# Expert stage of a two-block transformer kernel: instructions held in program order, one-hot tiles built in pairs two groups ahead

## The chip, the cores and the metric

The kernel runs on one core of one Trainium2 chip. The metric is device time in microseconds (us) of one execution. The engines are PE (TensorE, matrix products; PEld is its loading of weights), DVE (VectorE), ACT (ScalarE), POOL (GpSimd) and SP (SyncE, which here only issues DMAs). DMAs issued by SP go through queue q1, those issued by POOL through queue q0.

## The reference, cut to what matters

The program computes a first block (convolution and windowed attention, then a PEER expert layer) and a second block of two layers. Only the expert layer of the first block is touched:

```python
def peer(h, w_pq, sub_keys, u_emb, v_emb):
    ...
    s_top, i_top = lax.top_k(sc, PEER_TOPK)
    cand = s_top[..., 0, :, None] + s_top[..., 1, None, :]
    ...
    best, pos = lax.top_k(cand, PEER_TOPK)
    expert_idx = jnp.take_along_axis(cand_idx, pos, axis=-1)
    gate = jax.nn.softmax(best, axis=-1).astype(h.dtype)
    ...
    def chunk(args):
        hx, idx, g = args
        a = jax.nn.gelu(jnp.einsum("ced,cd->ce", u_emb[idx], hx), approximate=False)
        return jnp.einsum("ce,ced->cd", g * a, v_emb[idx])
```

There are 256 tokens, 8 heads with 16 chosen experts each (128 experts for a token), 16384 experts, and a width of 1024 in float32.

## The kernel before, in words

**Two ways for two sets of tokens.** 160 of the 256 tokens (N = 160) go the dense way: every expert is computed, and a mostly empty gate matrix picks the chosen ones. 128 blocks of 128 experts pass through `ublock`, which loads one tile of 512 KB of the first table (`ut`), multiplies it in 8 matmuls with the activations `hn`, and leaves gelu of the product in the tile `G`. In the same way 128 blocks of the second table (`vv`) are multiplied with G in `vmm`. The other 96 tokens go by rows: `RowGroup` fetches for each of 64 and then 32 steps a tile of 128 rows (512 KB) by an indirect DMA from POOL, `dot` multiplies it with the activations on DVE (first table), `axpy` adds it to a sum on DVE (second table). That is 192 row tiles: 96 of `un`, 96 of `vv`. `some_rows(RU)` after a U block and `some_rows(RV)` after a V block say how many steps of this come into the program per block; a row is used RB - 1 steps after its fetch.

**Three stretches.** First `ublock`s that alternate with what is left of the top-16 selection (`unit`, `select`, `gates`), which `pump` doles out to DVE by estimated costs; tokens 128 to 255 (tt = 1) come first, then tokens 0 to 127 (tt = 0). `gates` computes the softmax and, in `turn`, transposes indices and gates with PE; for tt = 1 `turn` also fills the row indices and sets `asked`, from which on rows are fetched. Second, the placing: for 40 groups of 4 tokens `onehots` builds one-hot tiles (QO on DVE, P and R from it on ACT), `place` multiplies them on PE (8 matmuls of 128 columns) into a gate tile in PSUM, and multiplies that gate into G (on DVE for the blocks already done, a copy on ACT for those to come). From then on a `ublock` multiplies its gelu with the gates already placed (`ac`, on DVE). Some two U blocks stand between groups. Third, the 128 V blocks, the last 5 of them interleaved with the adding of the row groups' sums.

**Order and buffers.** `whole` loads all blocks from SP into a ring of 10 tiles named raw, whi and wlo; a tile is free once PE has used its block. U products use 4 PSUM tiles ("mm"). A scheduler of the framework takes the program and decides the order on each engine; each engine then works strictly in that order.

Of the kernel before, what the change touches and what calls it, by code (L numbers as in the profile page):

```python
# [17 lines left out]
PSUM = bass.MemoryType.PSUM  # L18
DRAM = bass.MemoryType.DRAM
# [55 lines left out]
RU = 0.68  # L75
RV = 0.8

# [7 lines left out]
RB = 6  # L85


class Kernel:
    def __init__(self, tc, a, dump=None):
        self.tc, self.nc, self.a = tc, tc.nc, a  # L90
        self.dump = dump or (lambda *k: None)
        self.es = ExitStack()
        self.pools = {}
        self.wt = 0
        self.bg = []
        self.credit = 0.0
        self.lag = []

# [700 lines left out]
    def peer(self):  # L799
# [11 lines left out]
        gTl = p2h.tile([128, T], F32, name="gTl")  # L811
# [118 lines left out]
        def gates(tt):  # L930
            at = lambda t: t[:, tt]
            nc.vector.scalar_tensor_tensor(at(ei), at(isel), float(N_KEYS), at(jsel), op0=ALU.mult, op1=ALU.add)
            nc.vector.tensor_tensor(at(ex), at(best), best[:, tt, :, 0:1].to_broadcast([128, 8, 16]), op=ALU.subtract)
            nc.scalar.activation(at(ex), at(ex), AF.Exp)
            sm = p2t.tile([128, 8], F32, name="sm", bufs=1)
            nc.vector.reduce_sum(sm, at(ex), axis=AX.X)
            nc.vector.reciprocal(sm, sm)
            nc.vector.tensor_mul(at(ex), at(ex), sm[:, :, None].to_broadcast([128, 8, 16]))
            ts = slice(tt * 128, (tt + 1) * 128)
# [12 lines left out]
            self.later(1, turn)  # L952
            yield 1.5
# [19 lines left out]
        def whole(src, n):  # L973
# [3 lines left out]
            nc.sync.dma_start(raw, src)  # L977
            return raw

        def G(i, t=slice(None)):  # L980
            return Gs[i // 64][:, i % 64, t]

        def ublock(i, n_t):
            raw = whole(a["ut"][i], i)
            pt = self.pp.tile([128, N], F32, name="mm", bufs=4)
            for k in range(C):
                nc.tensor.matmul(pt, raw[:, k * 128:(k + 1) * 128], hn[:, k, :N], start=(k == 0), stop=(k == C - 1))  # L987
            self.tick()
# [44 lines left out]
        done, i = 0, 0  # L1033
        while self.bg:
# [5 lines left out]
        for _ in range(2):  # L1040
            ublock(i, 0)
            some_rows(RU)
            i += 1
# [53 lines left out]
        for i in range(64 - LAST):  # L1097
            blk = (i, whole(a["vv"][i], nv))
# [422 lines left out]
class RowGroup:  # L1521
# [3 lines left out]
    def __init__(self, k, pool, hn, ei, ex, t0, n):  # L1525
# [5 lines left out]
        self.idx = pool.tile([128, n], I32, name=f"idx{t0}")  # L1531
        self.gate = pool.tile([128, n], F32, name=f"gate{t0}")
# [3 lines left out]
        nc.vector.reduce_sum(self.fold, k.ident.rearrange("p (c t) -> p t c", t=n), axis=AX.X)  # L1536

# [16 lines left out]
    def indices(self):  # L1554

        nc, k = self.k.nc, self.k
        tt = self.t0 // 128
        pt = k.pp.tile([128, 2, 128], F32, name="ax", bufs=4)
        for j, src in enumerate(self.src):
            nc.tensor.matmul(pt[:, j], self.spread, src[:, tt].rearrange("p a b -> p (a b)"), start=True, stop=True)  # L1560
        for c in range(self.copies):
            ps = slice(c * self.n, (c + 1) * self.n)
            nc.vector.tensor_copy(self.idx[ps], pt[ps, 0, ps])
            nc.vector.tensor_copy(self.gate[ps], pt[ps, 1, ps])
# [222 lines left out]
```

## Time and profile before

| what | value |
|---|---|
| three runs | 1698.18, 1698.95 (median), 1701.84 us |
| the profiled execution | 1699.78 us, its span 1698.0 us |
| PE, DVE, ACT, POOL busy | 93%, 68%, 40%, 25% of the span |
| mean granted TensorE clock | 0.968 |
| moved by DMA | 398.98 MB, 235 GB/s over the span |

The span is the time from the first to the last instruction of the profiled execution; 1.8 us lie around it. "Busy" for PE does not mean working at its peak. All times below that name a moment are microseconds from the span's start. The expert stage's U blocks begin at 344.3, its gate placing at 480.7, its V blocks at 754.3, and its last adding ends at about 1043.

### The profile page before, as it was taken

Reading aid. Unit: us, or ns where it says so; the run is one execution under the profiler, and the core shown is the slowest. Engines: PE = TensorE matmul, PEld = TensorE weight load, DVE = VectorE, ACT = ScalarE, POOL = GpSimd, SP = SyncE. Lnnn points to the kernel's source line nnn. Section 1 sums busy time; section 2 is a strip of 40 time slices with the busy share of each in tenths; the row PEclk is TensorE's granted clock in tenths of the full one; section 3 lists DMA queues with packets and bytes.
Section 4 is the critical chain, followed back from the end, with each engine's and each line's share of the span. In section 5 each row is a group of like instructions: output and inputs, shape, how many; then the busy total and the mean of one; then the engine's idle time right before and its main releaser. Section 6 shows DMA issues by size and latency. Waiting matters only on the chain.

```text
span 1698.0 us, 29932 instructions
## 1 busy us (share of the span) xinstructions
PE 1577.1 (93%) x11502; PEld 1488.8 (88%) x11502; DVE 1155.1 (68%) x2510; ACT 678.3 (40%) x1549; POOL 430.4 (25%) x308
## 2 busy tenths in 40 slices
PE   8989989979667898979999999999999999999998
PEld 7878879979667788879999999887999998799986
DVE  6989988999777888884500005965777666676754
ACT  4557545531144454420000004455555444554543
POOL 3734622604554556663300000100000011000000
PEclk9989989989879999999999999999999999999999
DMA  5523436548999999999997774642655567265553
GB/s 182 171 75 101 137 124 216 158 174 334 357 356 408 408 409 400 409 392 410 409 338 241 246 227 155 224 137 75 210 194 186 183 191 221 90 191 180 182 190 113
DMA packets 109390, 398.98 MB, mean 235 GB/s; under 512 B 12484, under 2 KB 12643, under 8 KB 108736
## 3 DMA queue, kind: packets, MB, share of 16 engines
q1 hardware_dynamic: 78336, 282.63, 48.7%
q0 software_dynamic: 30768, 114.39, 17.9%
q8 instruction: 90, 1.47, 0.4%
q14 instruction: 52, 0.43, 0.1%
q10 hardware_dynamic: 144, 0.07, 0.0%
HBM read 394.86 MB, written 6.11 MB: 236 GB/s over the span
## 4 chain that ended last, share of the span: by engine, by line
PE 60%; DVE 18%; DMA 14%; issue 4%; POOL 2%; ACT 1%; SPq 0%; DVEq 0%; POOLq 0%; ACTq 0%
PE ax L1077 14%; PE mm L147 11%; PE mm L148 11%; PE mm L149 11%; DMA row<-un,idx 6%; DMA row<-vv,idx 4%; PE mm L987 2%; DVE ax L591 2%; PE mm L215 1%; PE mm L213 1%; PE ax L444 1%; PE mm L214 1%; DVE junk L1573 1%; DVE acc L1583 1%; DMA wlo<-vv 1%
## 5 line engine op out<-in xcount | busy, mean ns | idle before, releaser
L124 ACT ACTIVATE whi<-raw 128x1024 fp32r<-128x1024 f32 x275 | 290.2, 1058 | 602.3 <-DMA raw<-wst 287.6
L128 DVE TENSOR_TENSOR wlo<-raw,whi 128x1024 fp32r<-128x1024 f32 x211 | 257.9, 1224 | 277.9 <-ACT whi L124 271.6
L147 PE MATMUL mm<-xgh,whi 128*128 128x256 f32 x1064 | 304.4, 286 | 0.0
L148 PE MATMUL mm<-xgl,whi 128*128 128x256 f32 x1064 | 301.5, 283 | 2.6 <-DVE xgl L387 2.6
L149 PE MATMUL mm<-xgh,wlo 128*128 128x256 f32 x1064 | 301.2, 283 | 0.4 <-DVE wlo L128 0.4
L148 PEld LDWEIGHTS mm<-xgl,whi 128*128 128x128 f32 x1064 | 202.2, 190 | 2.9 <-DVE xgl L387 2.8
L147 PEld LDWEIGHTS mm<-xgh,whi 128*128 128x128 f32 x1064 | 202.0, 190 | 1.1 <-issue 0.8
L149 PEld LDWEIGHTS mm<-xgh,wlo 128*128 128x128 f32 x1064 | 202.1, 190 | 0.7 <-DVE wlo L128 0.6
L126 POOL TENSOR_TENSOR wlo<-raw,whi 128x1024 fp32r<-128x1024 f32 x64 | 153.5, 2403 | 138.1 <-ACT whi L124 135.3
L1583 DVE SCALAR_TENSOR_TENSOR acc<-row,w,acc 128x1024 f32<-128x1024 f32 x94 | 120.8, 1285 | 62.5 <-DMA row<-vv,idx 62.1
L1568 POOL DMA_INDIRECT row<-un,idx x96 | 113.7, 1185 | 148.7 <-PE mm L987 57.0
L1568 POOL DMA_INDIRECT row<-vv,idx x96 | 121.6, 1266 | 107.1 <-DVE acc L1583 61.2
L1573 DVE CUSTOM_DVE_ANT_0 junk<-row,h 128x1024 f32<-128x1024 f32 x96 | 117.5, 1224 | 43.6 <-DMA row<-un,idx 39.0
L987 PE MATMUL mm<-hn,raw 128*128 128x160 f32 x816 | 125.5, 311 | 3.4 <-ACT G L995 3.1
L987 PEld LDWEIGHTS mm<-hn,raw 128*128 128x128 f32 x816 | 117.9, 198 | 8.9 <-ACT G L995 7.2
L1077 PE MATMUL ax<-G,raw 128*128 128x160 f32 x832 | 122.6, 300 | 0.2
L1077 PEld LDWEIGHTS ax<-G,raw 128*128 128x128 f32 x832 | 115.7, 190 | 0.8 <-DMA raw<-vv 0.7
L987 PE MATMUL mm<-hn,whi 128*128 128x160 f32 x624 | 96.4, 310 | 16.0 <-ACT G L990 11.0
L987 PEld LDWEIGHTS mm<-hn,whi 128*128 128x128 f32 x624 | 90.2, 197 | 22.9 <-ACT G L990 11.3
L148 PE MATMUL mm<-hl,whi 128*128 128x256 f32 x368 | 107.2, 291 | 2.2 <-DVE hl L358 2.1
L987 PE MATMUL mm<-hn,wlo 128*128 128x160 f32 x608 | 93.7, 309 | 15.8 <-ACT G L990 12.7
L987 PEld LDWEIGHTS mm<-hn,wlo 128*128 128x128 f32 x608 | 87.8, 197 | 20.0 <-ACT G L990 12.9
(433 smaller groups left out, 3430.7 us busy)
## 6 DMA issues: line engine op xcount, KB each, us to landing
raw<-wst SPq DMA_DIRECT2D x278, 512.0 KB
raw<-vv SPq DMA_DIRECT2D x52, 512.0 KB
raw<-ut SPq DMA_DIRECT2D x51, 512.0 KB
whi<-ut SPq DMA_DIRECT2D x39, 512.0 KB
wlo<-ut SPq DMA_DIRECT2D x38, 512.0 KB
wlo<-vv SPq DMA_DIRECT2D x38, 512.0 KB
whi<-vv SPq DMA_DIRECT2D x38, 512.0 KB
tabr<-tabd POOLq DMA_DIRECT2D x1, 2048.0 KB
```

The costliest lines, as they stand in the source:

```text
L124: nc.scalar.activation(hi, raw, AF.Copy)
L126: nc.gpsimd.tensor_sub(lo, raw, hi)
L128: self.pin = nc.vector.tensor_sub(lo, raw, hi)
L147: nc.tensor.matmul(pt, w[:, s], xs[0][:, k], start=first, stop=False)
L148: nc.tensor.matmul(pt, w[:, s], xs[1][:, k], start=False, stop=False)
L149: nc.tensor.matmul(pt, lo[:, s], xs[0][:, k], start=False, stop=last)
L591: nc.vector.scalar_tensor_tensor(y[:, c] if k == 30 else ps, u[:, c, k:k + T], cw[:, c, k:k + 1], ps, op0=ALU.mult, op1=ALU.add)
L987: nc.tensor.matmul(pt, raw[:, k * 128:(k + 1) * 128], hn[:, k, :N], start=(k == 0), stop=(k == C - 1))
L1077: nc.tensor.matmul(acc[d // 2][:, d % 2, :N], raw[:, d * 128:(d + 1) * 128], G(i), start=False, stop=False, skip_group_check=True)
L1568: self.k.nc.gpsimd.indirect_dma_start(t, None, table, bass.IndirectOffsetOnAxis(ap=self.idx[:, s:s + 1], axis=0))
L1573: self.k.nc.vector.tensor_tensor_reduce(junk, row, self.h, 1.0, 0.0, ALU.mult, ALU.add, self.a[:, s:s + 1])
L1583: self.k.nc.vector.scalar_tensor_tensor(self.acc, row, w, self.acc, op0=ALU.mult, op1=ALU.add)
```

## The change

Everything lies in the expert stage. A context `in_order` ties each instruction of an engine to the one before it in the program (an order without a semaphore), from the first `ublock` to the end of the V loop. RU goes from 0.68 to 0.8, the row buffers RB from 6 to 8. The steps of `gates` come 2, 3 and 4 blocks after its first two DVE operations (GL), the row indices (`pick(0)`) apart from the row gates (`pick(1)`). One-hots are built with two tokens next to each other in the innermost dimension; R is made by POOL in one operation for a group, no longer by 4 operations on ACT; they are built two groups ahead of their use. `put`, the second half of the old `place`, runs one block later, and the product with `ac` one block later too (3 `ac` buffers). Of the V blocks each one whose number is divisible by 4 is loaded from POOL, not SP.

```diff
-RU = 0.68
+RU = 0.8
...
+GL = (2, 3, 4)
...
-RB = 6
+RB = 8
...
+    @contextmanager
+    def in_order(self):
+        traced = self.nc.cur_bb.bb.instructions
+        start = traced[-1]
+        yield
+        traced = list(self.nc.cur_bb.bb.instructions)
+        n = next(k for k in reversed(range(len(traced))) if traced[k] is start)
+        last = {}
+        for ins in traced[n:]:
+            if ins.engine in last and ins.engine in PINNED:
+                self.tc.add_manual_dep(ins, last[ins.engine].name, mybir.DependencyInfo(
+                    mybir.DependencyClass.NoSync, mybir.DependencyReason.DATA), reason="in_order")
+            last[ins.engine] = ins
...
+            if tt == 1:
+                self.later(GL[0], ask)
+            for n, fn in zip(GL, (exp, softmax, turn)):
+                self.later(n, fn)
...
-                nc.vector.tensor_mul(G(i, slice(0, n_t)), G(i, slice(0, n_t)), ac[:, :n_t])
+                muls.append((G(i, slice(0, n_t)), ac[:, :n_t]))
...
-            QO = oh.tile([128, 2, NT, 128], F16, name="QO", bufs=3)
-            P, R = (oh.tile([128, NT, 128], F16, name=n, bufs=2) for n in ("P", "R"))
-            nc.vector.tensor_tensor(QO, io[:, None, None, :].to_broadcast([128, 2, NT, 128]),
-                                    jiT[:, :, ts, None].to_broadcast([128, 2, NT, 128]), op=ALU.is_equal)
+            QO = oh.tile([128, 2, NT // 2, 128, 2], F16, name="QO", bufs=3)
+            P, R = (oh.tile([128, NT // 2, 128, 2], F16, name=n, bufs=3) for n in ("P", "R"))
+            for p in range(NT // 2):
+                ps = slice(t0 + 2 * p, t0 + 2 * p + 2)
+                nc.vector.tensor_tensor(QO[:, :, p], io[:, None].to_broadcast([128, 2, 128, 2]),
+                                        jiT[:, :, None, ps].to_broadcast([128, 2, 128, 2]), op=ALU.is_equal)
             for k in range(NT):
-                for dst, g in ((P, gT), (R, gTl)):
-                    nc.scalar.activation(dst[:, k], QO[:, 1, k], AF.Copy, scale=g[:, t0 + k:t0 + k + 1])
...
+            nc.gpsimd.tensor_tensor(R, QO[:, 1], gTl[:, t0:t0 + NT].rearrange("p (a b) -> p a b", b=2)[:, :, None].to_broadcast([128, NT // 2, 128, 2]), op=ALU.mult)
...
+        ohs = [onehots(4 * g, poh, io) for g in range(2)]
+        done, pts = 0, []
         for g in range(n_g):
...
+            if g + 2 < n_g:
+                ohs.append(onehots(4 * (g + 2), poh, io))
+            while i < i0 + 1 + (g + 1) * (126 - i0) // n_g:
                 ublock(i, 4 * done)
                 some_rows(RU)
+                products(1)
                 i += 1
...
+            pts.append(place(4 * g, ohs.pop(0)))
...
-            blk = (i, whole(a["vv"][i], nv))
+            blk = (i, whole(a["vv"][i], nv, nc.gpsimd if nv % 4 == 0 else nc.sync))
```

**ACT at the start.** Rows of ACT around the two exponentials of `gates` (`ex`), between the gelu operations (`G<-mm`, one per U block), before:

```order
L934 ACTIVATE ex<-ex 128x128
L990 ACT_TABLE_LOAD
L990 ACTIVATE G_4197<-mm 128x160 x8
L949 ACTIVATE jiT<-ax 128x2x128
L950 ACTIVATE gT<-ax 128x128
L357 ACTIVATE gTh<-gT 128x128
L990 ACTIVATE G_4197<-mm 128x160 x13
L934 ACT_TABLE_LOAD
L934 ACTIVATE ex<-ex 128x128
```

The same place of the change:

```order
L1023 ACTIVATE G_4197<-mm 128x160 x11
L962 ACT_TABLE_LOAD
L962 ACTIVATE ex<-ex 128x128
L1023 ACT_TABLE_LOAD
L1023 ACTIVATE G_4197<-mm 128x160 x2
L976 ACTIVATE jiT<-ax 128x2x128
L977 ACTIVATE gT<-ax 128x128
L376 ACTIVATE gTh<-gT 128x128
L1023 ACTIVATE G_4197<-mm 128x160 x22
L962 ACT_TABLE_LOAD
L962 ACTIVATE ex<-ex 128x128
```

The first exponential stood behind 3 gelus and stands behind 11 now; the second stood 21 gelus later and stands 24 later now. On PE the products that need the row indices stand behind 11 U blocks before and 12 now, the second transposes behind 36 and 38, and the first placing behind 40 and 41.

**DVE in the placing.** Rows of DVE about two groups long (`junk` is a row's dot product, QO the one-hots, `G<-ax` the placed gates, `G<-G,ac` the product of a U block), before:

```order
L1573 ISA junk,a_4205<-row,h_4201 128x1024
L1573 ISA a_4205 128x1
L1023 SCALAR_TENSOR_TENSOR G_4197<-ax,G_4197 128x4x40
L1003 TENSOR_TENSOR QO<-io,jiT 128x1024
L1573 ISA junk,a_4205<-row,h_4201 128x1024
L1573 ISA a_4205 128x1
L996 TENSOR_TENSOR G_4197<-G_4197,ac 128x4
L1573 ISA junk,a_4205<-row,h_4201 128x1024
L1573 ISA a_4205 128x1
L1573 ISA junk,a_4205<-row,h_4201 128x1024
```

The change, with the one-hots of a group as two operations:

```order
L1035 TENSOR_TENSOR G_4197<-G_4197,ac 128x24
L1044 TENSOR_TENSOR QO<-io,jiT 128x2x256 x2
L1035 TENSOR_TENSOR G_4197<-G_4197,ac 128x28
L1068 SCALAR_TENSOR_TENSOR G_4197<-ax,G_4197 128x4x57
L1632 ISA junk,a_4206<-row,h_4201 128x1024
L1632 ISA a_4206 128x1
L1035 TENSOR_TENSOR G_4197<-G_4197,ac 128x28
L1044 TENSOR_TENSOR QO<-io,jiT 128x2x256 x2
L1632 ISA junk,a_4206<-row,h_4201 128x1024
L1632 ISA a_4206 128x1
```

A group had three or four dot products between its QO and the next one's; it has one or two now, each held between operations that wait for PE's blocks.

**POOL.** Rows of POOL from the last product of the selection (`eq`) to the second stretch of rows, before:

```order
L885 TENSOR_TENSOR eq<-eq,tops 128x1024
L1568 DMA row<-un,idx_4203 128x1024 x46
L1568 DMA row<-un,idx_4213 128x1024 x32
L1568 DMA row<-vv,idx_4203 128x1024 x61
L1093 DMA xo<-park 128x2048
```

The change at the start of the placing:

```order
L904 TENSOR_TENSOR eq<-eq,tops 128x1024
L1627 DMA row<-un,idx_4203 128x1024 x5
L1048 TENSOR_TENSOR R<-QO,gTl 128x512 x3
L1627 DMA row<-un,idx_4203 128x1024 x3
L1048 TENSOR_TENSOR R<-QO,gTl 128x512
```

And at the start of the V blocks:

```order
L1627 DMA row<-un,idx_4216 128x1024 x6
L1008 DMA wlo<-vv 128x1024
L1627 DMA row<-un,idx_4216 128x1024 x3
L1008 DMA wlo<-vv 128x1024
L1627 DMA row<-vv,idx_4203 128x1024 x4
L1008 DMA raw<-vv 128x1024
```

40 operations R and 31 loads of V blocks now stand between the row fetches, at which POOL waits for DVE's one-hots and for PE's blocks. 93 of the 192 row fetches stand ahead of the first V block on POOL, 99 behind it.

## Rows read from the trace of the kernel before

**Rows 1.** Busy time by stage: start, placing, V with rows, V without.

```profile
core 0: us, PE busy (x) PEld busy (x) DVE busy (x) ACT busy (x) POOL busy (x), PEclk, DMA share, GB/s
344.30:480.70 136.40, 96.76 (x689) 95.92 (x688) 115.97 (x435) 24.68 (x61) 50.11 (x40) 0.86 0.80 297
480.70:754.30 273.60, 234.32 (x1732) 221.31 (x1732) 232.12 (x382) 132.38 (x549) 160.99 (x120) 0.96 1.01 399
754.30:855.00 100.70, 99.99 (x712) 98.37 (x713) 51.84 (x43) 0.18 (x1) 36.72 (x37) 0.98 1.01 402
855.00:1043.00 188.00, 188.00 (x1396) 188.00 (x1395) 8.46 (x17) 7.66 (x16) 0.00 (x0) 1.00 0.71 237
```

**Rows 2.** Waits of PE at the start, 344 to 490: total us, times, longest.

```profile
PE mm L987 <- ACT G L990: 23.7, 2, 12.7
PE ax L1017 <- ACT P L1007: 15.8, 1, 15.8
```

**Rows 3.** Waits of all engines in the placing, 480 to 755.

```profile
ACT G L1025 <- DVE G L1023: 124.6, 37, 10.1
...
DVE junk L1573 <- DMA row<-un,idx: 25.1, 25, 1.3
```

**Rows 4.** DMA queues from 344 to 755: packets, MB, share of 16 engines.

```profile
q0 software_dynamic: 22239, 81.01, 50.3%
q1 hardware_dynamic: 18822, 68.51, 43.2%
```

**Rows 5.** PE in order of time: start, us; after the waits, and one placing.

```profile
374.45 4.43 PE L987 MATMUL mm<-hn,whi 128*128 128x160 f32 x16 [11.01 <-ACT G L990]
...
482.99 4.58 PE L987 MATMUL mm<-hn,raw 128*128 128x160 f32 x16
...
489.74 0.22 PE L1017 MATMUL ax<-P,QO 128*128 128x128 f16 x1
...
490.13 0.22 PE L1017 MATMUL ax<-R,QO 128*128 128x128 f16 x1
```

**Rows 6.** First DVE operation of the stage's program, by its line.

```profile
L1536 DVE TENSOR_REDUCE fold<-ident x2: 278/327/376, 360.9 to 361.2; 128x64 f32<-128x128 f32 x1, 128x32 f32<-128x128 f32 x1
```

**Rows 7.** DVE in order of time: a dependent chain, selection, the two gate indices, dots.

```profile
15.06 0.16 DVE L339 SCALAR_TENSOR_TENSOR rr<-rt,rr 128x2 f32<-128x2 f32 x1
15.25 0.35 DVE L338 SCALAR_TENSOR_TENSOR rt<-rv,rr 128x1 f32<-128x1 f32 x2
...
382.25 0.29 DVE L822 FIND_INDEX8 iu<-tv,sc 128x8 uint32<-128x128 f32 x1
382.45 0.27 DVE L932 SCALAR_TENSOR_TENSOR ei<-isel,jsel 128x128 f32<-128x128 f32 x1
...
442.92 0.29 DVE L932 SCALAR_TENSOR_TENSOR ei<-isel,jsel 128x128 f32<-128x128 f32 x1
443.13 1.22 DVE L1573 CUSTOM_DVE_ANT_0 junk<-row,h 128x1024 f32<-128x1024 f32 x1
...
444.39 1.22 DVE L1573 CUSTOM_DVE_ANT_0 junk<-row,h 128x1024 f32<-128x1024 f32 x1
```

**Rows 8.** DVE groups of the stage, 330 to 1030: busy us, mean ns.

```profile
L1003 DVE TENSOR_TENSOR QO<-io,jiT 128x1024 f16<-128x1024 f16 x40 | 48.7, 1222 | 0.0
L1023 DVE SCALAR_TENSOR_TENSOR G<-ax,G 128x256 f32<-128x256 f32 (+6 forms) x68 | 32.9, 527 | 0.0
L996 DVE TENSOR_TENSOR G<-G,ac 128x16 f32<-128x16 f32 (+39 forms) x88 | 21.2, 241 | 0.0
L881 DVE TENSOR_TENSOR eq<-f,iota 128x1024 f32<-128x1024 f32 x8 | 9.7, 1213 | 0.0
```

**Rows 9.** POOL in order of time: two products of the selection.

```profile
415.52 2.64 POOL L885 TENSOR_TENSOR eq<-eq,tops 128x1024 f32<-128x1024 f32 x1
...
422.05 3.39 POOL L885 TENSOR_TENSOR eq<-eq,tops 128x1024 f32<-128x1024 f32 x1 [0.55 <-DVE eq L881]
```

**Rows 10.** DVE in the same time.

```profile
415.87 2.37 DVE L877 TENSOR_TENSOR f<-f 128x64 f32<-128x64 f32 x1
...
423.17 2.42 DVE L867 CAST f<-q 128x256 f32<-128x256 uint32 x1
```

**Rows 11.** Waits of SP's DMA queue in the stage, 344 to 1045.

```profile
SPq L977 <- PE mm L987: 285.3, 94, 22.3
```

More of the change, by code (lines that the diff above doesn't have):

```diff
@@ L1 @@
 import math
-from contextlib import ExitStack, nullcontext
+from contextlib import ExitStack, contextmanager, nullcontext
 from itertools import zip_longest
@@ L18 @@
 PSUM = bass.MemoryType.PSUM
+ET = mybir.EngineType
+PINNED = (ET.PE, ET.DVE, ET.Activation, ET.Pool, ET.SP)
 DRAM = bass.MemoryType.DRAM
@@ L931, in gates, with ask, exp, softmax @@
             at = lambda t: t[:, tt]
+            ts = slice(tt * 128, (tt + 1) * 128)
+            sm = p2t.tile([128, 8], F32, name="sm", bufs=2)
             nc.vector.scalar_tensor_tensor(at(ei), at(isel), float(N_KEYS), at(jsel), op0=ALU.mult, op1=ALU.add)
             nc.vector.tensor_tensor(at(ex), at(best), best[:, tt, :, 0:1].to_broadcast([128, 8, 16]), op=ALU.subtract)
[L934 to L939, printed above, removed]
+            def ask():
+                for g in rows:
+                    g.pick(0)
+                asked.append(tt)
+            def exp():
+                nc.scalar.activation(at(ex), at(ex), AF.Exp)
+            def softmax():
+                nc.vector.reduce_sum(sm, at(ex), axis=AX.X)
+                nc.vector.reciprocal(sm, sm)
+                nc.vector.tensor_mul(at(ex), at(ex), sm[:, :, None].to_broadcast([128, 8, 16]))
             def turn():
@@ L1016, in place, with put @@
                     k = (t0 + t) % NT
-                    nc.tensor.matmul(pt[:, t], QO[:, 0, k], P[:, k], start=P is Ps[0], stop=P is Ps[-1])
+                    nc.tensor.matmul(pt[:, t], Q[:, k // 2, :, k % 2], P[:, k // 2, :, k % 2], start=P is Ps[0], stop=P is Ps[-1])
+            return pt
+        def put(t0, n_i, pt):
             for k in range(2):
@@ L1032, in peer @@
         self.bg += [select(0, 0, nc.gpsimd), select(0, 4, nc.gpsimd), gates(0)]
-        done, i = 0, 0
-        while self.bg:
+        order = self.in_order()
+        order.__enter__()
+        i = 0
+        while self.bg or self.lag:
             ublock(i, 0)
@@ L1039, in peer @@
             i += 1
[L1040 to L1043, printed above, removed]
         self.close("p2t")
@@ L1097, in peer @@
         for i in range(64 - LAST):
-            blk = (i, whole(a["vv"][i], nv))
+            blk = (i, whole(a["vv"][i], nv, nc.gpsimd if nv % 4 == 0 else nc.sync))
             nv += 1
@@ L1104, in peer @@
             pass
+        order.__exit__(None, None, None)
         pw = self.open("pw", side="right")
@@ L1536, in __init__ @@
         nc.vector.reduce_sum(self.fold, k.ident.rearrange("p (c t) -> p t c", t=n), axis=AX.X)
+        self.own = pool.tile([128, self.copies], F32, name=f"own{t0}")
+        nc.vector.reduce_sum(self.own, k.ident.rearrange("p (c t) -> p c t", t=n), axis=AX.X)
         self.spread = pool.tile([128, 128], F32, name=f"spread{t0}")
@@ L1552, in activations, with pick @@
             nc.scalar.activation(self.h[:, half * 512:(half + 1) * 512], pt, AF.Copy)
-    def indices(self):
+    def pick(self, j):
         nc, k = self.k.nc, self.k
[L1557 to L1564, printed above, removed]
+        pt = k.pp.tile([128, 128], F32, name="ax", bufs=4)
+        nc.tensor.matmul(pt, self.spread, self.src[j][:, self.t0 // 128].rearrange("p a b -> p (a b)"), start=True, stop=True)
+        t = self.pool.tile([128, self.n, self.copies], F32, name="own", bufs=1)
+        nc.vector.tensor_tensor(t, pt.rearrange("p (c s) -> p s c", s=self.n),
+                                self.own[:, None, :].to_broadcast([128, self.n, self.copies]), op=ALU.mult)
+        nc.vector.reduce_sum((self.idf, self.gate)[j], t, axis=AX.X)
+        if j == 0:
+            nc.vector.tensor_copy(self.idx, self.idf)
     def row(self, table, s):
```

51 lines of the change are left out of this document (29 added, 22 removed).

## The prediction

> **What bounds the kernel now.** I read the busy time by stage first. The expert stage takes 344.3 to 1043, 699 of 1698 us, and no stretch of it is like the next [rows 1]. In the last one PE works all the time: 1396 matmul instructions in 188.0 us, 0.1347 us each; a block is 8 float32 products of two instructions each, so 16 x 0.1347 = 2.155 us. The DMA there runs at 237 GB/s. In the placing the DMA runs at 399 GB/s, in the V blocks with rows at 402, so these look like the most it gives, and PE is kept waiting in the placing: 87 blocks and 320 small products fill 273.6 us. So the stage has rows ahead of PE's pace while PE is short of data, and half a DMA idle when only PE is left. In the start the reverse holds: DVE is busy for 116.0 of 136.4 us and PE sits at a mean clock of 0.86.
>
> Second, the waits. At the start PE waits three times, 11.0, 12.7 and 15.8 us [rows 2]: ACT stands at an exponential, or at P, that needs DVE's selection, and the gelus behind it free no PSUM. [...] In the placing the longest wait is ACT's for DVE's placed gates, 124.6 us, and DVE in turn waits 25.1 us for rows [rows 3]: dots stand ahead of the gates on DVE, so a late row holds up DVE, then ACT, then PE. Third, the DMA queues: rows on q0 moved 81.0 MB while blocks on q1 moved 68.5 MB [rows 4], so rows took more than half of the DMA while PE was short of blocks.
>
> **The change, part 1: the start.** Compare at equal work, 41 U blocks and one placing. Before, that ends at 482.99 + 4.58 = 487.6 [rows 5]. After, PE can't be first: the index products stand behind block 12 and the transposes of tt = 0 behind block 38, and both need DVE. So I add up DVE. Its first operation of the stage was at 360.9 behind 792 others [rows 6]; it stands behind 776 now, 16 at 0.18 each: 358. The 0.18 comes from the trace: 67 instructions from 360.9 to the end of the first gate index at 382.7 [rows 6, 7], ten of them wide (1.21 less an overlap of some 0.08 [rows 8], 1.14), leave 57 for 10.4 us. Now 73 stand there, 12 wide: 13.7 + 61 x 0.18 = 24.7. What the pin costs: operations that need the one just before them. In selection 0.29 us operations that the scheduler mixed from two units start 0.20 apart; a dependent 0.16 us operation starts 0.19 behind the other [rows 7], so a dependence costs 0.03 more than the duration where mixing gives 0.09 back: 0.12. 42 of the 73 wait for DVE itself: 5.0. The index of tt = 1 is ready at 388; PE's 12 blocks are 25.9 of the 44 us from 344.3, so PE waits.
>
> To the index of tt = 0 before: 163 instructions in 60.5 us [rows 7], of them 13 dots (1.15 between others) and 8 wide, 142 small at 0.18; that is 49.7, and 10.8 went in waits, POOL's products among them. After, the same number with 10 dots and 87 dependences: 11.5 + 9.1 + 145 x 0.18 + 87 x 0.12 + 10.8 = 67.9, so 456, plus 1 for the index products; PE's 26 blocks from 388 (4.4 + 25 x 2.155 = 58) end at 446, so it waits again. Softmax and transposes take 2.5; then three blocks, the first at the low clock (4.4 + 2 x 2.155 = 8.7), beside which DVE makes six QO, ACT the first P, POOL the first R. First placing: 468.7, so **-18.9 us**. If dependences cost nothing it is 15 better; if POOL's 10.8 doubles, 11 worse.
>
> **Part 2: the placing.** What is left is 87 blocks in 40 groups, 2.175 blocks and (x 0.8) 1.74 rows for each. Before it took 754.3 - 487.6 = 266.7. After, for one group: PE 2.175 x 2.155 + 0.44 for a placing [rows 5] = 5.13. DMA 3.915 x 0.5243 MB at 0.402 MB per us = 5.11. DVE: dots start 1.26 apart [rows 7], 2.19; the `ac` products 2.175 x (0.241 - 0.08) = 0.35; placed gates 68 for 40 groups at 0.527 - 0.08, 0.76 [rows 8]; the one-hots, which no row shows in the new form: 1.222 us for 1024 elements [rows 8], so at the same rate two of 512 with a fixed part of 0.16 each (the smallest of [rows 7]; 0.16 + 512 x 1.04 ns = 0.69, less 0.08) 1.22; no gain from pairs gives this, and half the time per element would give 0.69. I take the old operation's rate, the nearest row. The new R on POOL: the nearest row is POOL's product of 1024 elements, 2.64 us [rows 9], so 1.3 for 512. While it ran, DVE's 64-element add took 2.37 us and a cast 2.42 [rows 10], and POOL's own second one 3.39, behind DVE. [...] Sum for DVE 5.42, more than PE's 5.13: DVE bounds. 40 x 5.42 = 216.8, **-49.9 us**. ACT loses 160 copies and is not near it (132 of 274 busy). That nothing is lost to order: one-hots are two groups ahead, some 10 us, `ac` has three buffers and PSUM four, so DVE may be some four blocks late before PE sees it; rows have seven steps, 19 us, to land.
>
> [...]
>
> **Part 3: V blocks.** Before: 288.7 us, of which 128 x 2.155 = 276 blocks, 13 the adding and its sums. After: 99 rows, 118 blocks that the ring of ten has not yet taken and 1 MB of `xo` are 114.8 MB, at 402 GB/s 285.6 us. PE alone would still do 276. So DMA bounds, between 0 and 9.6 worse; as PE and DMA both ran full at 0.8 rows and 402 GB/s before [rows 1] and the last rows stand behind the last loads, I take **+8 us**. What hid rows before, idle DMA after 855, is now used up to the end.
>
> SP's queue waited 285.3 us for PE to free tiles [rows 11], so a load from POOL costs nothing as long as POOL gets to it in time; behind it on POOL stand rows, which DVE waits for, and nothing else needs POOL.
>
> **Sum.** -18.9 - 49.9 + 8 = -60.8 on the profiled execution's 1699.8 (0.85 above the median of the three): **1639 us**. The rest of the kernel has the same instructions in nearly the same order.
>
> **Rivals.** A: R and DVE lock each other out. If R is as slow as the whole-size product, 2.64, and all of it comes off DVE, a group is 7.16 and the placing 286.4, 19.7 longer than before: 1699.8 - 18.9 + 19.7 + 8 = 1709, slower; it decides from 2.2 us per R on. [Rows 9, 10] speak for it, POOL's half-size operand against it. A milder form, 0.5 to 1.2 us more a group, gives 1659 to 1687.
>
> [...]
>
> B: POOL's queue gets half of the DMA at best, as [rows 4] show when both queues have work. Then V's 131 loads on it and `xo`, 69.7 MB at 201 GB/s, take 347 us, +58 in place of +8: 1689. Against it: SP has only 0.75 of a block to load per block and its ring is then full, so q1 must run dry.
>
> [...]
>
> C: the pace does nothing, since DMA's rate sets the placing anyway, and V stays: only the start is won, 1681. If the dependences eat that too, no change. Against it: U's bytes with 0.8 rows need 5.11 a group, and it took 6.7.
>
> **Chances.** Forecast, 1610 to 1660: 0.66. Milder A: 0.10. A: 0.08. B: 0.05. C with the start 0.06, without it 0.05. The forecast, the milder A, B and C with the start are faster by over 0.2% (about what this measurement can tell from no change): 0.87; 0.05 the same; A 0.08 slower. The range: the best case has PE as the bound (-12), V as before (-8) and cheap dependences (-10), 1609; the upper end takes in the milder A and C, 1685.
>
> **What will show it.** Right: first placing near 469, V from about 685 and to 980; PE's three early waits gone but two of some 12; ACT's wait for placed gates a small part of 124.6; DMA near 400 GB/s through V. Wrong: R over 2 us and long DVE operations beside it (A); PE waiting in V for tiles loaded by POOL with the DMA under 400 (B); dots that still wait for rows (C); the selection's small operations more than 0.3 apart, which moves the start.

## The result and the profile after

The changed kernel takes 1648.91 us (median of four runs, 1647.98 to 1652.05), the kernel before 1699.07 beside it: a ratio of 0.9705, 95% interval 0.9688 to 0.9723. That is 50.2 us less. The forecast was 60.8 less, 1639 us, with a range from 1609 to 1685; the time is inside it, and the forecast's direction held, but 10 us of the gain are missing, and one term hides more than that.

The profiled execution spans 1647.4 us. Its stages, for [rows 1] (the same columns; the V part is cut around one stop):

```profile
core 0: us, PE busy (x) PEld busy (x) DVE busy (x) ACT busy (x) POOL busy (x), PEclk, DMA share, GB/s
343.70:465.00 121.30, 99.49 (x712) 98.53 (x712) 108.32 (x407) 29.37 (x75) 39.36 (x28) 0.90 0.78 282
465.00:677.70 212.70, 209.33 (x1707) 207.60 (x1704) 179.32 (x375) 98.28 (x372) 146.86 (x112) 1.00 1.00 390
677.70:820.00 142.30, 137.17 (x964) 135.65 (x964) 69.82 (x66) 0.23 (x1) 71.93 (x66) 0.96 1.01 399
820.00:842.00 22.00, 11.87 (x75) 11.63 (x76) 5.21 (x5) 0.00 (x0) 9.03 (x11) 0.76 0.85 321
842.00:991.00 149.00, 146.32 (x1072) 145.57 (x1070) 66.82 (x63) 7.53 (x15) 60.14 (x53) 0.99 0.93 366
```

The first block behind the first placing starts at 465.0. The zeros, the four products with a tile of zeros that open the sums of the V part, come at 677.7. So the start is 22.6 us shorter, the placing takes 212.7 in place of 266.7 (54.0 less), and V, which ends at 991.0, takes 313.3 in place of 288.7 (24.6 more). The rest is 1.4 longer. In the placing TensorE is busy for 209.3 of 212.7 us at full clock, DVE for 179.3 only, and the DMA runs at 390 GB/s.

The waits of PE at the start, for [rows 2]:

```profile
PE ax L1617 <- DVE ei L953: 13.0, 1, 13.0
PE ax L975 <- DVE jsel L906: 4.6, 1, 4.6
PE ax L975 <- DVE ex L967: 4.2, 1, 4.2
```

and of all engines in the placing, for [rows 3]:

```profile
ACT G L1070 <- DVE G L1068: 39.5, 39, 1.9
...
DVE QO L1044 <- PE ax L1058: 17.4, 21, 2.1
```

ACT's wait for placed gates fell from 124.6 to 39.5 us, the dots' wait for rows is gone, and DVE now waits for PE: it asks for the next one-hots' buffers before PE has used them. The groups of DVE in the placing, for [rows 8]:

```profile
L1632 DVE CUSTOM_DVE_ANT_0 junk<-row,h 128x1024 f32<-128x1024 f32 x70 | 86.7, 1238 | 0.1
L1035 DVE TENSOR_TENSOR G<-G,ac 128x16 f32<-128x16 f32 (+37 forms) x84 | 43.8, 522 | 0.1
...
L1044 DVE TENSOR_TENSOR QO<-io,jiT 128x512 f16<-128x512 f16 x74 | 28.1, 420 | 17.7 <-PE ax L1058 17.4
```

A comparison of 512 elements takes 420 ns where 1024 took 1222; the products `G<-G,ac` take 522 in place of 241.

In V one stop is plain. POOL stands at the load of `xo` until PE has let go of the memory that `xo` is put in, with a block's load behind it (in order of time: start, us, ..., and in brackets the idle time before and its end):

```profile
829.73 0.56 POOL L1147 DMA_DIRECT2D xo<-park  x1 [19.12 <-PE ax L1130]
830.28 0.57 POOL L1008 DMA_DIRECT2D wlo<-vv  x1
```

PE gets that block 9 us later, and it takes 4.64 us in place of 2.34; the granted clock was 0.50 from 839.0 to 843.6:

```profile
839.09 4.64 PE L1130 MATMUL ax<-G,wlo 128*128 128x160 f32 x16 [9.99 <-DMA wlo<-vv]
843.52 2.75 PE L1130 MATMUL ax<-G,raw 128*128 128x160 f32 x13
```

And V has a tail. The last two rows' sums run on DVE at 972.2, the first product of the adding comes right behind, and the next stage begins 18.8 us after the first of them:

```profile
972.19 2.60 DVE L1642 SCALAR_TENSOR_TENSOR acc<-row,w,acc 128x1024 f32<-128x1024 f32 x2 [1.17 <-DMA row<-vv,idx]
```

```profile
975.28 0.53 PE L1646 MATMUL ax<-fold,acc 128*128 128x64 f32 x4
...
990.96 0.36 PE L166 MATMUL mm<-xgh,whi 128*128 128x256 f32 x1
```

### The profile page after: what moved, and what is told of

Read it like the earlier page. It is cut to its first block, busy times and chain, and to the rows that moved or that the text cites. A ratio compares the mean times of both kernels' runs of the same rounds, so it can differ in the third digit from the quotient of the medians.

```text
span 1647.4 us, 29860 instructions
## 1 busy us (share of the span) xinstructions
PE 1563.3 (95%) x11502; PEld 1485.5 (90%) x11502; DVE 1176.5 (71%) x2549; ACT 649.1 (39%) x1387; POOL 509.9 (31%) x379
## 4 chain that ended last, share of the span: by engine, by line
PE 71%; DVE 17%; DMA 7%; issue 3%; POOL 2%; ACT 1%; SPq 0%; POOLq 0%; DVEq 0%; ACTq 0%
PE ax L1130 12%; PE mm L1020 12%; PE mm L166 11%; PE mm L167 11%; PE mm L168 11%; DMA raw<-vv 3%; DMA wlo<-vv 3%; DVE ax L610 2%; PE mm L234 2%; PE mm L232 1%; PE mm L233 1%; PE ax L463 1%; DVE wlo L147 1%; PE ax L1058 1%; PE ax L1376 1%
## 5 line engine op out<-in xcount | busy, mean ns | idle before, releaser
L1627 POOL DMA_INDIRECT row<-un,idx x96 | 110.0, 1146 | 108.2 <-DVE idf L1621 54.3
L1020 PE MATMUL mm<-hn,raw 128*128 128x160 f32 x816 | 118.8, 300 | 0.0
L1020 PEld LDWEIGHTS mm<-hn,raw 128*128 128x128 f32 x816 | 112.8, 190 | 0.0
L1130 PE MATMUL ax<-G,wlo 128*128 128x160 f32 x608 | 93.5, 307 | 11.0 <-DMA wlo<-vv 11.0
L1130 PEld LDWEIGHTS ax<-G,wlo 128*128 128x128 f32 x608 | 88.1, 196 | 12.1 <-DMA wlo<-vv 11.9
L610 DVE SCALAR_TENSOR_TENSOR ax<-u,cw,ax 128x256 f32<-128x256 f32 x227 | 97.7, 481 | 0.7
L166 PE MATMUL mm<-hh,whi 128*128 128x256 f32 x304 | 90.3, 297 | 2.7 <-DVE u L630 2.2
## 6 DMA issues: line engine op xcount, KB each, us to landing
wlo<-vv POOLq DMA_DIRECT2D x13, 512.0 KB, 16.5
```

The lines of the kernel that those rows point to most:

```text
L166: nc.tensor.matmul(pt, w[:, s], xs[0][:, k], start=first, stop=False)
L610: nc.vector.scalar_tensor_tensor(y[:, c] if k == 30 else ps, u[:, c, k:k + T], cw[:, c, k:k + 1], ps, op0=ALU.mult, op1=ALU.add)
L1130: nc.tensor.matmul(acc[d // 2][:, d % 2, :N], raw[:, d * 128:(d + 1) * 128], G(i), start=False, stop=False, skip_group_check=True)
L1627: self.k.nc.gpsimd.indirect_dma_start(t, None, table, bass.IndirectOffsetOnAxis(ap=self.idx[:, s:s + 1], axis=0))
```

## The experiments

Every one was timed beside the kernel before. "Placing" is from the first placing to the zeros (the last of them, where they lie apart), "V" from there to the first product of the next stage, both in the profiled execution, in us. What runs ahead of the placing is the same program in most of these kernels and still ends anywhere from 464.2 to 470.1, so lengths of stages are compared, and medians. In the four kernels with the same V blocks (after, qo_old, r_act, ahead0) V took 313.2 to 314.9.

| run | median | ratio to before | 95% | placing | V |
|---|---|---|---|---|---|
| before | 1699.07 | 1 | | 273.4 | 288.7 |
| after | 1648.91 | 0.9705 | 0.9688-0.9723 | 213.2 | 313.2 |
| xo_act | 1647.47 | 0.9692 | 0.9676-0.9709 | 213.2 | 310.0 |
| vv_sp | 1646.39 | 0.9687 | 0.9671-0.9703 | 213.2 | 309.6 |
| skip16 | 1638.46 | 0.9654 | 0.9638-0.9671 | 213.2 | 301.1 |
| rv1 | 1669.43 | 0.9830 | 0.9812-0.9847 | 213.2 | 332.9 |
| pin_dve | 1669.52 | 0.9834 | 0.9817-0.9852 | 213.2 | 332.4 |
| nopin | 1757.48 | 1.0354 | 1.0333-1.0374 | 322.2 | 295.7 |
| before_pin | 1710.39 | 1.0066 | 1.0051-1.0082 | 267.5 | 321.2 |
| qo_old | 1652.31 | 0.9729 | 0.9713-0.9745 | 212.8 | 314.6 |
| r_act | 1649.16 | 0.9715 | 0.9694-0.9735 | 213.2 | 314.1 |
| ahead0 | 1652.09 | 0.9727 | 0.9712-0.9742 | 213.2 | 314.9 |
| ru9 | 1641.39 | 0.9658 | 0.9645-0.9672 | 209.5 | 305.7 |
| ru9_sp | 1637.90 | 0.9640 | 0.9627-0.9653 | 209.5 | 306.9 |

Two questions were open: why V lost three times what was forecast, and which part of the change made the placing.

**V: is it the stop at `xo`?** (xo_act)

```
-        nc.gpsimd.dma_start(xo, park)
+        nc.scalar.dma_start(xo, park)
```

> Only the load of xo moves, from POOL's queue to ACT's, which has nothing else to do in the V blocks. Theory 1 (POOL's order): in the changed kernel POOL stands 19.1 us at this load, a vv block's load stands behind it, and PE then waits 10.0 us and runs a block of 4.64 in place of 2.34. Without that stop the time falls by 9 to 13 us from 1648.9, to 1636 to 1640, and no PE wait over 4 us is left in V. Rival (the DMA's rate sets V): the two slices with less than 409 GB/s around the stop hold some 4 us of it; the time falls by 0 to 4 us, and PE's wait comes back elsewhere in V.

V is 3.2 us shorter, and the median falls by 1.4, in intervals that overlap: the rival. The stop of 10 us is gone, and PE's waits in V are still 14 us in sum, now in eight short ones, the longest 3.8:

```profile
PE ax L1130 <- DMA raw<-vv: 8.9, 5, 3.8
PE ax L1130 <- DMA wlo<-vv: 5.3, 3, 2.3
```

With the DMA at 409 GB/s on both sides of it (755 to 820 and 842 to 900 in the changed kernel), the stop was mostly given back: 10.0 us of wait cost V 3.2.

**Is it the blocks' loads behind rows on POOL's queue?** (vv_sp)

```
-            blk = (i, whole(a["vv"][i], nv, nc.gpsimd if nv % 4 == 0 else nc.sync))
+            blk = (i, whole(a["vv"][i], nv))
```

> All loads of vv blocks go on SP's queue, as before the change; the load of xo stays on POOL with its wait, and only rows stand behind it. Theory 1 (POOL's order): blocks never stand behind rows or xo, so both the stop of 10.0 us with its slow block and the waits at the start of V (3.8 and 3.0) go: 15 to 21 us less than 1648.9. Rival (the queues share): rows run ahead on their own queue and take up to half of 408 GB/s, so a block needs 0.524 MB at 204, 2.57 us, against PE's 2.155, for as long as rows last; V is as long as now or up to 5 us longer, and PE waits a little at very many blocks loaded by SP.

V is 3.6 shorter: between the two, nearer to the rival. The long waits went, and in their place many blocks take a little longer (27.3 blocks in the 65 us from 755, 2.38 each). But the run moves more than the loads. With rows alone ahead of it POOL issues one every 2.56 us up to 792, which is 205 of the 409 GB/s, as the rival had it; then it stands at `xo`:

```profile
836.92 0.58 POOL L1147 DMA_DIRECT2D xo<-park  x1 [43.62 <-PE ax L1130]
```

So this run doesn't take the queue apart from the stop. With either of the two edits V still stands some 13 us above the forecast.

**Is it the bytes?** (skip16)

```
-            blk = (i, whole(a["vv"][i], nv, nc.gpsimd if nv % 4 == 0 else nc.sync))
+            blk = (i, blk[1] if nv % 8 == 7 else whole(a["vv"][i], nv, nc.gpsimd if nv % 4 == 0 else nc.sync))
```

> Leaves out the loads of 16 of the 128 V blocks (every eighth; TensorE multiplies by the block before once more), so the V part is not the reference's. All work of the engines stays. Theory 1 (bytes: V lasts until its bytes have gone through at 408 GB/s, and the adding comes behind that): 16 x 0.524 MB at 0.408 MB per us, 20.6 us less than 1648.9, 1626 to 1632; PE's own 276 + 13 would stop it at 24 less. Rival (PE's stops set V: the load behind xo, loads behind rows on POOL, blocks at the low clock): 0 to 6 us less.

In the two loops that the edit touches 15 loads are left out (105 loads of blocks behind the zeros in place of 120), not 16, so the first theory's number is 19.3 and not 20.6. V is 12.1 shorter: neither number. The reading that fits is that with fewer bytes PE's own pace comes up, and that its stops then count in full. The waits of PE in V:

```profile
PE ax L1130 <- DMA wlo<-vv: 7.1, 1, 7.1
...
PE ax L1130 <- DMA raw<-vv: 3.4, 1, 3.4
```

The wait at `xo` alone is 7.1 here, and two slow blocks (4.12 and 3.84 in place of 2.34, in windows granted 0.91 and 0.84) add 3.3. PE's 276 + 13 with these 13.8 is 302.8, and 301.1 was measured. So the same stop costs 3 us while the DMA is the bound and, by this sum and not by a run, some 9 when PE is.

**Is it the tail?** (rv1)

```
-RV = 0.8
+RV = 1.0
```

> One number: 1.0 rows with each V block in place of 0.8, so the rows end with block 99 in place of 123. The bytes are the same. Theory 1 (bytes, and then a tail: the last row landed at 972 and the adding with the last blocks took 18.8 us more, with the DMA nearly empty): the DMA's last bytes are now blocks, V ends some 10 us behind them and not 19, and PE's pace of 289 is the other bound: 8 to 18 us less than 1648.9. Rival (the tail is in the program's order anyway, and earlier rows only starve PE earlier): 0 to 5 us more.

20.5 us slower, on neither side, and the most useful miss. The stretch with rows, and the one after them:

```profile
679.80:936.00 256.20, 219.97 (x1540) 214.33 (x1540) 130.58 (x114) 0.23 (x1) 136.15 (x126) 0.97 1.01 398
936.00:1012.80 76.80, 75.85 (x569) 75.85 (x569) 10.88 (x19) 7.52 (x15) 2.11 (x4) 1.00 0.63 217
```

With rows, 1540 products are 96 blocks in 256 us, 2.66 each: a block and a row are 2 x 0.5243 MB at 0.409 MB per us, 2.56. Behind the rows, PE is at its own pace of 0.135 a product and the DMA at 217 GB/s. On POOL each fourth block's load stands behind the rows that the program wrote ahead of it, so blocks can't run far ahead of rows. With the same bytes V is 19.7 longer, so it is not its bytes over 409 GB/s. What fits is a sum over blocks: (1 + r) x 1.282 us for a block with r rows, 2.155 for one without, and 13 for the rest of V (what it took beyond its blocks before the change). For r = 1: 99 x 2.564 + 29 x 2.155 + 13 = 329.3, and 332.9 was measured. For r = 0.8: 123 x 2.308 + 5 x 2.155 + 13 = 307.7; 313.2 was measured, and 310.0 without the stop at `xo`.

**Which part made the placing? The order on DVE alone** (pin_dve; the `in_order` of the change, with fewer engines)

```
-PINNED = (ET.PE, ET.DVE, ET.Activation, ET.Pool, ET.SP)
+PINNED = (ET.DVE,)
```

> The pinned order on DVE alone; PE's order comes out the same, ACT, POOL and SP are left to the scheduler, which on POOL moves some rows past R. Theory 1 (what the pin does is DVE's order: one-hots and placed gates ahead of dots whose rows are late): 1645 to 1660. Rival (POOL's order does it, rows kept from running ahead): the placing goes back to 250 or more, 1690 to 1757.

The time is on neither side, because the two stages part: the placing is whole, 213.2, as the first theory has it, and V is 332.4. Both in rows:

```profile
465.90:678.60 212.70, 209.32 (x1707) 207.60 (x1704) 179.63 (x377) 98.51 (x374) 139.11 (x113) 1.00 1.01 395
678.60:1011.00 332.40, 302.80 (x2108) 299.46 (x2109) 141.45 (x132) 7.69 (x16) 138.21 (x128) 0.96 0.91 353
```

So DVE's order is enough for the placing. The 19 us of V come from the order of the engines left free, and by their rows from POOL's: left to itself, POOL's queue gets mostly four or five rows between two loads of V (96 rows in 22 such gaps, 1.09 a block) where the pinned one has three or four, and ends with loads alone. The same sum gives 88 x 2.09 x 1.282 + 40 x 2.155 + 13 = 335.

**The change without the order** (nopin)

```
-        order = self.in_order()
-        order.__enter__()
...
-        order.__exit__(None, None, None)
```

> The program of the changed kernel without the pinned order: the scheduler decides again. It then sets 3 rows between two R on POOL where the pinned program has 1.74 on average. Theory 1 (order and pace made the gain): a group of the placing needs (2.175 + 3) x 0.5243 MB at 0.402, 6.75 us, the placing is 270 us in place of 212.7, the V blocks have few rows left and take some 289 in place of 313, and the start loses up to 15: 1680 to 1700. Rival (the cheaper one-hots and R on POOL made it): DVE is as light as in the changed kernel, and the time stays within 10 us of 1648.9.

1757, slower than the kernel before by 3.5% and far above both numbers. The placing takes 322 us, and not for the DMA's sake alone, as the first theory had it:

```profile
479.70:800.00 320.30, 245.17 (x1715) 234.34 (x1714) 239.81 (x423) 89.07 (x386) 215.25 (x172) 0.90 0.93 348
```

The DMA moves 348 GB/s and PE is granted 0.90; at 409 GB/s the same bytes would need 273 us, about the 270 of that theory. DVE, in order of time, shows the cause: each dot waits for its row, and the one-hots and placed gates that PE needs stand behind it.

```profile
574.54 1.23 DVE L1629 CUSTOM_DVE_ANT_0 junk<-row,h 128x1024 f32<-128x1024 f32 x1 [2.91 <-DMA row<-un,idx]
...
579.36 1.23 DVE L1629 CUSTOM_DVE_ANT_0 junk<-row,h 128x1024 f32<-128x1024 f32 x1 [1.20 <-DMA row<-un,idx]
580.50 0.08 DVE L1629 DVE_READ_ACCUMULATOR2_ANT a<- 128x1 f32 x1
...
581.18 0.63 DVE L1068 SCALAR_TENSOR_TENSOR G<-ax,G 128x256 f32<-128x256 f32 x1
```

**The order without the rest** (before_pin: the same `in_order`, in the kernel before)

```
+        order = self.in_order()
+        order.__enter__()
         done, i = 0, 0
         while self.bg:
...
         for _ in fetch:
             pass
+        order.__exit__(None, None, None)
```

> The kernel before with the pinned order alone, on all engines, in the order in which its program is written; nothing else is changed. Theory 1 (the pin is what gains): dots no longer stand ahead of the placed gates, and most of the 50 us come: 1680 or less. Theory 2 (the pin gains only with a program made for it): in the old program the placed gates stand right behind the placing on DVE and wait for PE, the next one-hots stand behind them, and eight copies on ACT behind those; the chain of a group is 1.1 + 1.2 + 2 + 0.4 and the dots besides, about what a group takes now: 1690 to 1730.

1710, the second theory. The start gains 14.9 us (first placing at 465.8) and the placing 5.9, at 267.5. On ACT eight copies of one-hots, 0.29 us apart, stand ahead of the gelu:

```profile
576.04 0.40 ACT L1025 ACTIVATE P<-QO,gT 128x128 f16<-128x128 f16 x1 [0.54 <-DVE QO L1021]
...
578.10 0.39 ACT L1025 ACTIVATE R<-QO,gTl 128x128 f16<-128x128 f16 x1
578.39 0.21 ACT L1011 ACTIVATE ac<-mm 128x72 f32<-128x72 f32 x1
```

and DVE, behind its one-hot, waits for that gelu 40 times, 2.6 us each:

```profile
574.79 1.22 DVE L1021 TENSOR_TENSOR QO<-io,jiT 128x1024 f16<-128x1024 f16 x1
578.63 0.23 DVE L1014 TENSOR_TENSOR G<-G,ac 128x72 f32<-128x72 f32 x1 [2.63 <-ACT ac L1011]
```

The loss lies in V, 32.5 us longer than before. POOL issues 113 rows behind the zeros there, where the scheduler's order left 36, and the DMA is full nearly to the end:

```profile
733.30:1054.50 321.20, 309.37 (x2109) 289.82 (x2109) 155.15 (x155) 7.73 (x16) 108.64 (x114) 0.99 0.99 390
```

So the order alone costs 0.7%, the other edits alone cost 3.5%, and both together gain 3%.

**One-hots in the old layout** (qo_old: one comparison of 1024 elements, all tiles without pairs)

```
-            for p in range(NT // 2):
-                ...
+            nc.vector.tensor_tensor(QO, io[:, None, None, :].to_broadcast([128, 2, NT, 128]),
+                                    jiT[:, :, t0:t0 + NT, None].to_broadcast([128, 2, NT, 128]), op=ALU.is_equal)
```

> The one-hots in the old layout, one comparison of 1024 elements a group in place of two of 512 in pairs; all else is as in the changed kernel. It adds some 0.5 us of DVE a group (1.22 against 0.74 for the two that overlap). Theory 1 (PE sets the placing, DVE has 0.8 us a group to spare): 0 to 4 us longer than 1648.9. Rival (DVE sets it, as the prediction had it): 40 x 0.5 = 20 us longer.

**R back on ACT** (r_act; `gTl` is float32 there, and the zeros are half as wide)

```
-            nc.gpsimd.tensor_tensor(R, QO[:, 1], gTl[:, t0:t0 + NT].rearrange("p (a b) -> p a b", b=2)[:, :, None].to_broadcast([128, NT // 2, 128, 2]), op=ALU.mult)
+                for dst, gg in ((P, gT), (R, gTl)):
+                    nc.scalar.activation(dst[:, k // 2, :, k % 2], QO[:, 1, k // 2, :, k % 2], AF.Copy, scale=gg[:, t0 + k:t0 + k + 1])
```

> R back on ACT, four more copies a group, so that POOL does nothing in the placing but issue rows (the zeros that open the accumulators are 256 wide in place of 512, to make room). Theory 1 (PE sets the placing): the products G<-G,ac fall from 517 to some 250 ns, 87 of them, R's lock is gone, and DVE is only idle for longer: within 4 us of 1648.9. Rival (DVE and the lock set it, as the prediction had it): 87 x 0.27 = 23 us less. A third way, ACT too late with gelus: it has 98 of 212 us busy and gets some 40 more, so no.

**One-hots at the group's own start** (ahead0)

```
-        ohs = [onehots(4 * g, poh, io) for g in range(2)]
+        ohs = []
...
-            if g + 2 < n_g:
-                ohs.append(onehots(4 * (g + 2), poh, io))
+            ohs.append(onehots(4 * g, poh, io))
```

> The changed kernel with each group's one-hots written at the group's own start, as before the change, and not two groups ahead. Theory 1 (in a pinned queue the one-hots stand behind dots, products and gates of blocks that PE is already past): PE waits at each placing for R or P, 0.5 to 1 us a group: 20 to 40 us more than 1648.9. Rival (the 4.7 us of a group's own blocks cover QO 0.74, P 4 x 0.23 and R 1.66): 0 to 5 us more.

All three leave the placing where it is, at 212.8 to 213.2; the medians are 0 to 3.4 us higher, in intervals that overlap with the changed kernel's. In qo_old DVE is busy 192.0 of 208.6 us, and PE still doesn't wait ahead of the zeros; in r_act the products are back at

```profile
L1035 DVE TENSOR_TENSOR G<-G,ac 128x16 f32<-128x16 f32 (+37 forms) x84 | 19.7, 234 | 0.2
```

and DVE is only idle for longer. For one-hots, R and the distance ahead, each taken back alone, PE's pace is the answer. The first theory held in the first two and failed in the third, where the rival did.

**A kernel that keeps the DMA full** (ru9)

```
-RV = 0.8
+RV = 0.74
...
-                some_rows(RU)
+                some_rows(0.9)
...
-        nc.gpsimd.dma_start(xo, park)
+        nc.scalar.dma_start(xo, park)
```

and the two memsets of the zeros moved to group 5 of the placing.

> The changed kernel with 0.9 rows a block in the placing (0.8 in the start as it was), 0.74 with a V block, xo loaded from ACT, and the zeros made early. The DMA moved 390 GB/s in the placing against 409 in V, so some 8 rows fit there. Theory 1 (a V block with r rows takes the larger of 2.155 and (1 + r) x 1.285 us): placing 212 to 217, V 123 x 2.236 + 10.8 + 13 and some 3 of waits = 302 in place of 313: 1636 to 1645. Rival (stops and queue order set V): V stays at 308 or more, and the rows moved into the placing only make that longer: 1646 to 1655.

1641.39, 7.5 us below the changed kernel, with intervals that don't touch: the first theory's time. The placing takes 3.7 us less (the wait of 3.4 for the zeros is one part) with the DMA at 404 GB/s:

```profile
467.90:677.00 209.10, 209.10 (x1709) 207.62 (x1706) 189.38 (x387) 96.34 (x370) 160.17 (x119) 1.00 1.02 404
677.00:982.70 305.70, 289.17 (x2111) 287.00 (x2109) 132.76 (x120) 8.09 (x18) 135.71 (x120) 0.98 0.97 383
```

V is 3.7 longer than that theory had it. Loads and rows issued in V and `xo` are 213 transfers, 111.7 MB, but 114.4 MB went through (117.0 less five weights of the next stage): 2.7 MB were still on their way at the zeros, 6.5 us. By this count the rows put into the placing were in part only queued there.

**And with V's first four POOL loads on SP** (ru9_sp)

```
+            blk = (i, whole(a["vv"][i], nv, nc.gpsimd if nv % 4 == 0 and nv > 143 else nc.sync))
```

> The kernel of the run with 0.9 and 0.74 rows a block, with the first four V blocks that POOL loaded now loaded by SP. There PE stood 9.55 us at the first of them, which POOL asked for at 675.9, behind rows whose buffers DVE had not freed, and then ran a block of 4.13. Theory 1 (a load behind rows in POOL's queue comes late, and PE with few rows a block is near its own pace): 8 to 11 us less than 1641.4, 1630 to 1634. Rival (bytes set V, and the wait comes back later): 1638 to 1643.

1637.90, at the edge of the rival's numbers and far from the first theory's. The wait of 9.55 us at V's start is gone and V is no shorter:

```profile
674.90:981.80 306.90, 291.72 (x2111) 285.80 (x2110) 132.77 (x120) 8.07 (x18) 135.53 (x117) 1.00 0.96 382
```

PE waits 13.5 us in thirteen small pieces, where ru9 had 15.9 in six. The 3.5 us to ru9 are not explained by V; 2 of them lie ahead of the first placing, and the intervals touch. Both kernels beat the two that were compared.

## Why the prediction held, and where it didn't

**The start: right.** Forecast 18.9 us less, measured 22.6. The first DVE operation of the stage's program ran at 357.5 (forecast 358), the index of the first unit at 386.3 (388), that of the second at 451.4 (456). PE's three waits of 11.0, 12.7 and 15.8 became one of 13.0 and two of 4.6 and 4.2. The forecast put 4.4 us for the first block behind such a wait, "at the low clock". In the trace of before that is the 4.43 of [rows 5], at a granted clock of 0.54 (374.4 to 378.9); in the changed kernel these blocks took 4.08 at 0.54 (386.7 to 391.6) and 3.74 at 0.60 (456.6 to 460.2). That it is the order, and not the other edits, two runs show: the first placing comes at 465.8 with the order alone and at 479.7 with all but the order.

**The placing: the size right, 54.0 against 49.9, but the bound wrong.** The sum had DVE at 5.42 us a group and PE second with 5.13. DVE is busy 179.3 us, 4.48 a group. Two terms were too large. QO is 0.76 a group, 0.68 less the overlap, and not 1.22. And the 5.42 holds 0.90 for R on POOL, beside 2.19, 0.35, 0.76 and 1.22 for DVE's own operations: no run shows that term. Measured, R takes 0.59 a group off DVE (84 products, each 281 ns dearer). PE bounds with 5.32 a group: 87 blocks of 2.17 and the 39 placings left of 0.46 are 207, the zeros' wait is 3.4, and 2 are left. That 5.32 lies so near to the forecast 5.42 is luck. The prediction's other value for QO, half the time per element, was 0.69, and its best case had PE as the bound; the trace shows 0.68 and PE busy for 209.3 of 212.7 us. The faster QO was worth nothing here: the run with the old layout shows PE not waiting for it either.

Why the order gains is argued from the dots in the prediction, and the runs bear it out: with the scheduler's order dots stand ahead of one-hots and placed gates, DVE waits 46 us for the dots' rows and 31 for those of the sums, and the placing is 322 long; with DVE's order pinned and no other engine's, 213. One thing that the order does there is to move rows. POOL's fetches from the first placing to the zeros, before and then after:

```profile
L1568 POOL DMA_INDIRECT row<-vv,idx x60 | 85.4, 1424 | 55.2 <-DVE G L996 32.4 <-DVE acc L1583 13.6 <-issue 3.3
L1568 POOL DMA_INDIRECT row<-un,idx x60 | 75.6, 1259 | 58.1 <-DVE G L996 30.5 <-DVE a L1573 20.6 <-issue 5.5
```

```profile
L1627 POOL DMA_INDIRECT row<-un,idx x73 | 83.8, 1148 | 25.1 <-issue 11.0 <-DVE a L1632 5.5 <-DVE G L1035 4.8
```

The old placing moved 109 MB, 267 us at 409 GB/s: with 120 rows in it the DMA alone would have held it near its length. The new one moves 83 MB, 203 us. The 47 rows that left went to V, where the DMA had run at 237 GB/s for 188 us and where POOL now issues 99 rows in place of 36; the start gave up the others. With DVE's order alone pinned 72 rows are left in the placing, with no order 129. But moving rows is not enough: the order alone leaves 59, the DMA runs at 291 GB/s, and the placing is 267.5 long.

That the order needs a program that is written for it was not foreseen; the prediction costed the edits one by one, and the order only in the start. Which of the edits it needs is open: three were taken back one at a time at no cost, the products and placed gates that come one block later were not tried.

**V: the mechanism in part, the size wrong.** This is the term that was mis-sized: "+8 us", measured 24.6. "DMA bounds, between 0 and 9.6 worse" set 285.6 of DMA against PE's 276, with the same 13 of adding behind either. The DMA's part holds: 123 blocks with 0.8 rows are 221 transfers, 283.9 us at the 409 GB/s of V. But 99 rows at 0.8 a block end with block 123, so five more blocks come behind them at PE's pace, 10.8 us, which a comparison of two totals leaves out. With the 13 that gives 307.7. (The 13 is not all adding: from the end of block 123 to the next stage both kernels take 17.0, that is 6.2 beyond five blocks; the rest lies in the zeros, the first blocks of V and a pace of 2.17.) The second failed step is "nothing else needs POOL": `xo` did, and its stop costs 3.2. 310.9 of 313.2 is so accounted for. The other 2.3 may lie at V's first blocks, where PE waits 3.8 for a load that POOL issues behind rows; no run took that apart from the rest.

**The rivals.** A: R takes 1.69 us in the mean, below the 2.2 from which it would have decided; R and DVE did hold each other up (below), and DVE had the room. B: PE does wait in V for tiles that POOL loads, which land 16.5 us after their issue against 7.5 from SP, but with SP loading them all V is only 3.6 shorter, in a run that moved `xo`'s stop as well. C: the dots no longer wait, so the pace counts. Summed, 3.7 and 4.1 gained beyond the forecast and 16.6 and 1.4 lost leave 10.2, so part of V's error is hidden by the other two stages.

## What to carry to other kernels

When each engine's order is fixed, a queue that two streams share can hold them at the program's ratio: 0.8 rows a block here. With the blocks on SP's queue a row went out every 2.56 us, about one a block: in the order alone, at the same 0.8 in the program, 30 rows and 31 blocks from 820 to 900. V is then a sum over blocks of the larger of PE's time and the block's own transfers, and moving rows earlier made it longer, because the DMA stood half empty after them (217 GB/s behind the rows of rv1, 409 full). Cost what is left behind the last transfer as a term of its own. And an order and the edits made for it are one change: measured apart, each lost time, the order in V and the edits in the placing.

## What the runs showed of the hardware

**Dots and products on DVE and R on POOL held each other up.** R starts at 560.21 while a dot runs:

```profile
560.21 1.86 POOL L1048 TENSOR_TENSOR R<-QO,gTl 128x512 f16<-128x512 f16 x1 [0.22 <-DVE QO L1044]
```

```profile
559.96 1.22 DVE L1632 CUSTOM_DVE_ANT_0 junk<-row,h 128x1024 f32<-128x1024 f32 x1
...
561.10 1.06 DVE L1035 TENSOR_TENSOR G<-G,ac 128x72 f32<-128x72 f32 x1
...
562.81 0.23 DVE L1035 TENSOR_TENSOR G<-G,ac 128x72 f32<-128x72 f32 x1
```

R of 512 elements takes 1.86 here. Where R began first (nopin), it took 1.04, and the dot that began 0.09 us behind it took 2.03 in place of 1.23:

```profile
565.03 1.04 POOL L1048 TENSOR_TENSOR R<-QO,gTl 128x512 f16<-128x512 f16 x1 [1.84 <-DVE QO L1044]
```

```profile
565.12 2.03 DVE L1629 CUSTOM_DVE_ANT_0 junk<-row,h 128x1024 f32<-128x1024 f32 x1 [0.26 <-DMA row<-un,idx]
```

In the changed kernel the product that came at 561.10 ended 0.1 us behind R and took 1.06, the next one 0.23. So in these cases whichever came second was held up for some 0.8 us: R by 0.82, the dot by 0.80, the product by 0.83. To this kernel the waits cost nothing: with R on ACT the placing is 213.2 too.

**What the stop at `xo` cost.** POOL's stop at `xo` led to a wait of 10.0 us in the changed kernel and of 7.1 in skip16. Taking the first away gave 3.2 us of V; the second is worth some 9 by the sum worked out there, an estimate. The block behind it took 4.64 us and 3.84 in place of 2.34; the granted clock was 0.50 from 839.0 to 843.6 in the changed kernel, and 0.84 from 820 to 842 in skip16.
